# Router logits summed quarter by quarter from rows not yet normalised, with the first tiles routed apart

## The chip, the cores and the metric

The kernel runs on one core of one Trainium2 chip. The time is the device time of one execution in microseconds (us). An engine works through its own instructions in the order of the program: PE is TensorE, DVE is VectorE, ACT is ScalarE, POOL is GpSimd and SP is the queue that issues the direct DMAs. PEld is the loading of a matmul's stationary operand. PEclk is the clock of TensorE that was granted, as a share of full speed.

## What is computed

One step of a hybrid decoder layer for a prompt of 512 rows and 8 sample rows, all of width 1024. A mixing sublayer and a memory cross-attention come first. The change concerns the seam between the cross-attention's output projection, the layer norm behind it, and the routing of the mixture of experts. From the reference, cut to that:

```python
hp = layer_norm(ALPHA * hp + cross_attention(hp, mk_p, mv_p, w_xq[l], w_xo[l]), ln2_g[l], ln2_b[l])
hp = layer_norm(ALPHA * hp + hier_moe(hp, *moe_w), ln3_g[l], ln3_b[l])
...
def hier_moe(h, w_grp, b_grp, w_rtr, b_rtr, w_e_gate, w_e_up, w_e_down):
    grp_logits = jnp.einsum('td,dg->tg', t, w_grp)                 # 4 groups
    g_idx = jnp.argmax(grp_logits + b_grp, axis=-1)
    p_g = jnp.take_along_axis(jax.nn.softmax(grp_logits, axis=-1), g_idx[:, None], axis=1)
    e_logits = jnp.einsum('td,de->te', t, w_rtr)                   # 4 x 8 experts
    ...                                                            # top 2 inside the group g_idx
    for e in range(N_EXPERTS):
        he = jax.nn.silu(t @ w_e_gate[e]) * (t @ w_e_up[e])
        y = y + gates[:, e:e + 1] * (he @ w_e_down[e])
```

The logits of a row are 36 numbers: 4 of groups and 32 of experts. The 32 experts' weights are 192 units of 512 KB and are read once.

## The kernel before

The 520 rows are five tiles: 0 to 3 are the prompt's rows, 128 each, and 4 holds the 8 sample rows. The work is written as generators ("streams") that a planner interleaves by an estimate of TensorE's time: a stream yields the time, or the condition, from which it may go on, and among those that may, the one of the lowest priority number goes first. The planner's choice is the order of the program, and so the order on every engine.

`out_proj("wxo", ...)` (L1354) projects the cross-attention's output through `natural` (L416). It goes through four quarters q of 256 output columns. In each it takes the sample rows first (8 matmuls in full float32, two passes each) and then tiles 0 to 3, with 24 matmuls each in a reduced format of float32 (the operands are split into a high and a low part, so three products for each of 8 slices of the contraction). `put` adds the residual and takes the statistics of the quarter. After the last quarter of a tile, `finish(t)` normalises the tile on VectorE (`normalize`, L1344), stores its rows to the DRAM buffer `h2d` and adds a stream `rate(t)`.

`rate(t)` (L1652) makes the logits of one tile: eight transposes of the normalised rows in two PSUM banks, two copies to SBUF (ScalarE and VectorE), eight matmuls with the 36 router columns `wrt`, which accumulate in one bank, and two additions of biases (`logits` for the weights of the experts, `biased` for the choice). When all five tiles are rated the streams end and the routing follows in one piece for all tiles:

```python
    o = first_max(eb4, 4, 8)
    ...
    V.tensor_tensor(h, og4, o, op=OP.mult)     # one-hot of the k-th expert of each row
    ...
    ixg = M([16], I32, keep=True)
    V.tensor_scalar(ixg, ps[:, :16], BIG, None, op0=OP.add)
    ...
    for pr in range(2):
        gather(pr)
    ...
    warm(2)
    turn(0)
```

`first_max` finds the first largest of each group, twice, on VectorE; an element of its operands is one expert of one tile, so 160 elements wide. Small matmuls count for each chosen expert how many rows stand ahead of this one (`pp`, `rank`), `placed` turns the ranks into a list `ixg` of row numbers for 16 pairs of experts, and `gather` (L1841) has POOL fetch the rows of a pair from `h2d` by an indirect DMA. `warm(n)` issues n matmuls whose results nobody uses. `turn(0)` transposes the gathered rows, and `gate_up(0)` multiplies them with the first pair's weights.

The experts' weights come in units of 512 KB (1024 columns). `prefetch` (L1627) issues a load for each free block of SBUF whenever blocks become free, in the order in which they are used. A last region (`arena_l`, nine units) becomes free when the projection's own buffers close. From `gate_up(0)` on, blocks are freed as the products use them up (`drop`), and the loads go on.

## Time and profile before

| what | value |
|---|---|
| median of 3 runs | 908.75 us (905.33 to 913.02) |
| the profiled execution, its time | 907.26 us |
| the profiled execution, its span | 905.5 us |
| mean granted clock of TensorE | 0.951 |
| busy share of the span: PE, DVE, ACT, POOL | 91%, 54%, 33%, 10% |
| chain that ended last, share by engine | PE 62%, DMA 22%, DVE 8%, ACT 3%, issue 2%, SPq 2% |
| read from HBM | 223.11 MB |

The time of the profiled execution lies 1.8 us above its span. A busy share is a mean over stages with different limits. The chain names what released each step, going back from the last instruction.

### The profile page before, as it was taken

The page shows a single profiled execution, that of the slowest core. Times are in us where ns is not written, and L with a number is a line of the kernel's source. Part 1 is how long each engine was busy: PE and PEld are TensorE (multiplying, and loading weights), DVE is VectorE, ACT ScalarE, POOL GpSimd, SP SyncE. Part 2 cuts the span into 40 slices and gives each one's busy share as a digit, 9 for nine tenths or more (in the row PEclk, how much of TensorE's full clock was granted, in tenths as well). Part 3 has the DMA queues.
Part 4 walks back from the last instruction along what each step waited for, and adds up shares of the span by engine and source line. Part 5 has one row for each costly group of instructions (what it writes and reads, how often), then busy time and mean ns, then how long its engine had stood idle before and what let it go on. Part 6 is the DMA issues. An engine that isn't in the chain of part 4 may idle for free.

```text
span 905.5 us, 17155 instructions
## 1 busy us (share of the span) xinstructions
PE 820.4 (91%) x6767; PEld 575.3 (64%) x6767; DVE 485.7 (54%) x1079; ACT 294.4 (33%) x616; POOL 87.5 (10%) x88
## 2 busy tenths in 40 slices
PE   6999989999997898999989989996899989989982
PEld 6998556666875786898768965995343434334331
DVE  5565356675557554533651675567453834625635
ACT  5422334352632433420442342121232403313311
POOL 4100101111320000000000001000310210200100
PEclk9999999999997987999979999998899999989997
DMA  7922696766793576688867346228699999999950
GB/s 265 310 80 79 178 281 203 247 196 230 231 350 132 192 256 233 228 307 318 268 218 278 98 162 209 84 107 313 209 409 411 412 409 410 408 409 409 409 210 24
DMA packets 83960, 230.43 MB, mean 254 GB/s; under 512 B 12482, under 2 KB 32988, under 8 KB 83492
## 3 DMA queue, kind: packets, MB, share of 16 engines
q1 hardware_dynamic: 74660, 203.98, 62.7%
q0 software_dynamic: 9216, 25.31, 8.0%
q8 instruction: 55, 0.90, 0.4%
q14 instruction: 29, 0.24, 0.1%
HBM read 223.11 MB, written 14.39 MB: 262 GB/s over the span
## 4 chain that ended last, share of the span: by engine, by line
PE 62%; DMA 22%; DVE 8%; ACT 3%; issue 2%; SPq 2%; POOL 0%; POOLq 0%; ACTq 0%; DVEq 0%
PE psd L219 33%; DMA arena_f<-in_we 10%; PE psm L219 9%; PE psx L219 9%; PE pss L219 7%; DVE arena_f L200 5%; DMA arena_d<-in_we 4%; PE psm L223 3%; DMA arena_l<-in_we 2%; DVE arena_r L200 2%; DMA arena_f<-in_latT 2%; ACT arena_f L200 2%; ACT arena_r L200 1%; SPq L239 1%; DMA arena_f<-in_wuq 1%
## 5 line engine op out<-in xcount | busy, mean ns | idle before, releaser
L219 PE MATMUL psd<-arena_r 128*128 128x256 f32 (+1 forms) x2208 | 295.9, 293 | 9.0 <-ACT arena_r L200 5.6
L219 PEld LDWEIGHTS psd<-arena_r 128*128 128x128 f32 x2208 | 281.7, 198 | 21.5 <-issue 9.3
L219 PE MATMUL psx<-arena_f 96*32 96x256 f32 (+1 forms) x728 | 132.7, 495 | 2.2 <-DMA arena_f<-in_latT 1.9
L200 DVE TENSOR_TENSOR arena_r<-arena_f,arena_r 128x1024 fp32r<-128x1024 f32 (+3 forms) x71 | 83.0, 1173 | 77.3 <-ACT arena_r L200 71.7
L200 ACT CAST arena_r<-arena_f 128x1024 fp32r<-128x1024 f32 (+3 forms) x73 | 71.2, 977 | 159.2 <-PE psd L219 118.7
L219 PE MATMUL psm<-arena_f 64*32 64x32 f32 (+10 forms) x1394 | 87.1, 282 | 14.4 <-DVE arena_f L200 9.4
L219 PE MATMUL pss<-arena_f 128*8 128x256 f32 (+5 forms) x466 | 92.3, 466 | 1.3 <-ACT arena_f L200 0.7
L219 PEld LDWEIGHTS psx<-arena_f 96*32 96x32 f32 (+1 forms) x728 | 43.9, 125 | 68.5 <-issue 51.9
L223 PE MATMUL psm<-cst,arena_f 128*128 128x128 f32 (+2 forms) x393 | 59.9, 280 | 19.8 <-DVE arena_f L200 5.4
L219 PEld LDWEIGHTS psm<-arena_f 64*32 64x32 f32 (+6 forms) x1384 | 47.6, 123 | 46.2 <-issue 22.5
L223 PEld LDWEIGHTS psm<-cst,arena_f 128*128 128x128 f32 (+2 forms) x393 | 44.0, 148 | 44.1 <-issue 20.4
L200 DVE TENSOR_TENSOR arena_f<-arena_f 128x1024 f32<-128x1024 f32 (+6 forms) x72 | 57.2, 827 | 7.5 <-ACT arena_f L200 3.6
L219 PEld LDWEIGHTS pss<-arena_f 128*8 128x8 f32 (+3 forms) x456 | 30.3, 121 | 37.8 <-issue 26.7
L200 DVE TENSOR_TENSOR arena_f<-arena_f,psx 128x256 f32<-128x256 f32 (+1 forms) x17 | 7.4, 432 | 86.9 <-ACT arena_f L200 86.9
L638 POOL DMA_INDIRECT arena_f<-in_latN,ixn x32 | 34.3, 1073 | 189.9 <-PE psm L219 176.2
L200 DVE SCALAR_TENSOR_TENSOR arena_f<-arena_f,psd 128x256 f32<-128x256 f32 (+2 forms) x60 | 28.6, 489 | 43.9 <-PE psd L219 34.6
L1841 POOL DMA_INDIRECT arena_f<-h2d,arena_s x24 | 26.2, 1092 | 220.8 <-PE psm L223 123.6
L200 ACT ACTIVATE arena_f<-psx 128x256 f32<-128x256 f32 x16 | 6.1, 384 | 122.8 <-PE psx L219 117.5
L219 PE MATMUL psx<-arena_d,arena_f 128*64 128x512 f32 x76 | 37.1, 676 | 9.4 <-DMA arena_d<-in_we 9.4
L219 PE MATMUL pss<-arena_l,arena_f 128*64 128x512 f32 x92 | 43.2, 593 | 0.0
L219 PE MATMUL psx<-arena_l,arena_f 128*64 128x512 f32 x92 | 35.7, 596 | 5.2 <-DMA arena_l<-in_we 5.2
L200 DVE SCALAR_TENSOR_TENSOR arena_m<-pss,arena_s,arena_m 128x512 fp32r<-128x512 f32 x32 | 23.7, 750 | 29.7 <-ACT arena_m L200 29.7
(212 smaller groups left out, 919.8 us busy)
## 6 DMA issues: line engine op xcount, KB each, us to landing
arena_f<-in_we SPq DMA_DIRECT2D x120, 512.0 KB, 10.6
arena_l<-in_we SPq DMA_DIRECT2D x46, 512.0 KB, 10.8
arena_f<-in_latT SPq DMA_DIRECT2D x128, 144.0 KB, 2.9
arena_d<-in_we SPq DMA_DIRECT2D x26, 512.0 KB, 11.1
arena_f<-in_wout SPq DMA_DIRECT2D x16, 512.0 KB, 5.5
arena_f<-in_wxq SPq DMA_DIRECT2D x16, 512.0 KB, 5.4
arena_f<-in_memKT SPq DMA_DIRECT2D x16, 512.0 KB, 5.3
arena_f<-in_memV SPq DMA_DIRECT2D x16, 512.0 KB, 5.2
```

The costliest lines, as they stand in the source:

```text
L200: return f(out, *args, **kw)
L219: return self.queue(self.eng.matmul(out, lhsT, rhs, **kw))
L223: return self.queue(self.eng.transpose(out, src, ident))
L239: return self.eng.dma_start(out, src)
L638: G.indirect_dma_start(out=out, out_offset=None, in_=src, in_offset=bass.IndirectOffsetOnAxis(ap=ix, axis=0))
L1841: G.indirect_dma_start(out=out, out_offset=None, in_=h2d, in_offset=bass.IndirectOffsetOnAxis(ap=ix, axis=0), bounds_check=NT - 1, oob_is_ ...
```

## The change

Four things change.

`rate(t, q)` now runs for each quarter of each tile, as soon as the quarter's residual is there. It transposes two blocks of the raw rows (not yet normalised), copies them to SBUF (ScalarE for even quarters, VectorE for odd ones), multiplies them with the two matching slices of `wrt` and adds the 36 sums into `logits`. The normalisation is put right afterwards: with mean m and reciprocal deviation r of a row, its logits are r times (raw sum minus m times the column sum of `wrt`) plus the bias. `prepare` makes the negative column sum (`moe["sum"]`) with eight more matmuls. At the last quarter the rows are normalised on ScalarE (Identity with scale and bias) instead of VectorE and stored.

The routing is split. `ORDER` is (0, 1, 4, 2, 3). A new stream `route()` waits until tile 3 is projected and tiles 0, 1 and 4 are rated, and chooses their experts (`choose(0, 3)`). The last step of tile 3's rating waits for that and emits the ranks of the first three tiles ahead of its own last logit matmuls. Behind the streams come `choose(3, 2)` for tiles 2 and 3 and their ranks, whose matmuls accumulate on the counts of the first three.

The bursts of warming matmuls are 2, 1 and 6 where there was one of 2.

A region of small buffers, `arena_s`, grows from 1400 to 1600 columns, and `arena_f` next to it loses none.

```diff
-COLS_S = 1400
+COLS_S = 1600
...
+            if then:
+                then(t, q)
...
+    ORDER = (0, 1, 4, 2, 3)
+    PLACE = [ORDER.index(t) for t in range(5)]
...
+    def rate(t, q):
         o, n = tiles5[t]
-        slots = moe["xt"].slots
-        if not slots:
-            yield lambda: slots
-        h2T = slots.pop(0)
-        for c in range(2):
-            ps = pm()
-            for k in range(4):
-                f = 4 * c + k
-                PE.transpose(ps[:, k * 128:k * 128 + n], res[t][:n, f * 128:(f + 1) * 128], ident[:n, :n])
-            to, p3 = h2T[:, 4 * c:4 * c + 4, :n], ps.rearrange("p (k n) -> p k n", k=4)[:, :, :n]
-            if c:
-                V.tensor_copy(to, p3)
-            else:
-                S.copy(to, p3)
-        yield PE.ready()
-        ps = ps_()
-        for k in range(8):
-            PE.matmul(ps[:n, :36], h2T[:, k, :n], moe["wrt"][:, k], start=k == 0, stop=k == 7)
-        V.tensor_add(biased[:n, t], ps[:n, :36], moe["bias2"][:n])
-        V.tensor_add(logits[:n, t], ps[:n, :36], moe["bias"][:n])
-        slots.append(h2T)
+        if "slots" not in moe or not moe["slots"]:
+            yield lambda: moe.get("slots")
+        h2T = moe["slots"].pop(0)
+        ps = pm()
+        for k in range(2):
+            f = 2 * q + k
+            PE.transpose(ps[:, k * 128:k * 128 + n], res[t][:n, f * 128:(f + 1) * 128], ident[:n, :n])
+        (V.tensor_copy if q % 2 else S.copy)(h2T[:, :, :n], ps[:, :256].rearrange("p (k n) -> p k n", k=2)[:, :, :n])
+        if q == 3:
+            mv, rs = moe["moments", t]
+            shift = stat.tile([128, 1], F32, tag="shift", name="shift", bufs=5)
+            V.scalar_tensor_tensor(shift[:n], mv[:n, 0:1], -1.0, rs[:n], op0=OP.mult, op1=OP.mult)
+            S.activation(res[t][:n], res[t][:n], AF.Identity, bias=shift[:n], scale=rs[:n])
+            Q.dma_start(h2d[o:o + n, :], res[t][:n])
+        yield PE.ready() if q == 3 else PE.now + 2.5
+        if q == 3 and "sum" not in done:
+            yield after("sum")
+        if (t, q) == (3, 3):
+            yield after("chosen")
+            ranks_of_first()
+        lg, p = moe["lg"][:n, t * 36:t * 36 + 36], PLACE[t]
+        if q == 3:
+            V.scalar_tensor_tensor(logits[:n, p], moe["sum"][:n], mv[:n, 0:1], logits[:n, p], op0=OP.mult, op1=OP.add)
+        for k in range(2):
+            PE.matmul(lg, h2T[:, k, :n], moe["wrt"][:, 2 * q + k], start=k == 0, stop=k == 1)
+        moe["slots"].append(h2T)
+        if q == 0:
+            V.tensor_copy(logits[:n, p], lg)
+        else:
+            V.tensor_add(logits[:n, p], logits[:n, p], lg)
+        if q < 3:
+            return
+        V.scalar_tensor_tensor(biased[:n, p], logits[:n, p], rs[:n], moe["bias2"][:n], op0=OP.mult, op1=OP.add)
+        V.scalar_tensor_tensor(logits[:n, p], logits[:n, p], rs[:n], moe["bias"][:n], op0=OP.mult, op1=OP.add)
         done.add(("rated", t))
-            normalize(t, 4)
-            Q.dma_start(h2d[o:o + n, :], res[t][:n])
-            streams.add(rate(t), -1, PE.now + 3.8)
-        yield from out_proj("wxo", columns2(hh, hl), xs, range(8), finish, lambda t: crossed)
+            moe["moments", t] = moments(t, 4)
+            done.add(("projected", t))
+        yield from out_proj("wxo", columns2(hh, hl), xs, range(8), finish, lambda t: crossed,
+                            lambda t, q: streams.add(rate(t, q), -1, PE.now + (0.0 if q == 3 else 2.5)))
...
+        moe["lg"] = ps_()
+        moe["slots"] = [xt[:, 2 * i:2 * i + 2] for i in range(4)]
+        yield PE.now + 9.0
+        ps = ps_()
+        for k in range(8):
+            PE.matmul(ps[:, :36], ones, moe["wrt"][:, k], start=k == 0, stop=k == 7)
+        V.tensor_scalar(moe["sum"], ps[:, :36], -1.0, None, op0=OP.mult)
+        done.add("sum")
...
+    def choose(a, m):
+        sl = slice(a, a + m)
+        b3 = biased[:, sl, 4:36]
+        b4 = b3.rearrange("p t (g e) -> p t g e", g=4)
+        for k in range(2):
+            o = first_max(b4, 4, 8, a, m)
+            if k == 0:
+                first_max(biased[:, sl, None, 0:4], 1, 4, a, m)
+                V.scalar_tensor_tensor(b3, o.rearrange("p t g e -> p t (g e)"), -3e38, b3, op0=OP.mult, op1=OP.add)
+            V.tensor_tensor(OH[k][:, sl].rearrange("p t (g e) -> p t g e", g=4), moe["og4"][:, sl], o, op=OP.mult)
...
+    def ranks(a, m):
+        sl = slice(a, a + m)
+        t32, rank = moe["t32"][:, sl], moe["rank"]
+        for k in range(2):
+            V.tensor_mul(t32, OH[k][:, sl], (moe["ahead"] if a else pp())[:, :m * 32].rearrange("p (t e) -> p t e", t=m))
+            V.reduce_sum(rank[:, sl, k], t32, axis=AX.X)
+            V.tensor_tensor(RR[k][:, sl], C("iota64")[:, None, :].to_broadcast([128, m, 64]),
+                            rank[:, sl, k:k + 1].to_broadcast([128, m, 64]), op=OP.is_equal)
+    def ranks_of_first():
+        ps = pp()
+        for k in range(2):
+            PE.matmul(ps[:, :96], moe["ub"], OH[k][:, :3].rearrange("p t e -> p (t e)"), start=k == 0, stop=False)
+            for p in range(3):
+                n = tiles5[ORDER[p]][1]
+                if p < 2:
+                    PE.matmul(ps[:, p * 32 + 32:96].rearrange("p (t e) -> p t e", e=32), moe["onesb"][:n],
+                              OH[k][:n, p:p + 1].to_broadcast([n, 2 - p, 32]), start=False, stop=k == 1 and p == 1)
+                PE.matmul(moe["ahead"][:, :64].rearrange("p (t e) -> p t e", e=32), moe["onesb"][:n],
+                          OH[k][:n, p:p + 1].to_broadcast([n, 2, 32]), start=k + p == 0, stop=False)
+        ranks(0, 3)
...
+    def route():
+        yield after(("projected", 3), *(("rated", t) for t in ORDER[:3]))
...
+        choose(0, 3)
+        for k in range(2):
+            carried(k, moe["tk"], 0, 3)
+        done.add("chosen")
...
+    placed_of(0, 3)
+    warm(2)
+    choose(3, 2)
+        PE.matmul(moe["ahead"][:, :64], moe["ub"], OH[k][:, 3:5].rearrange("p t e -> p (t e)"), start=False, stop=False)
+        PE.matmul(moe["ahead"][:, 32:64], moe["onesb"], OH[k][:, 3], start=False, stop=k == 1)
+    warm(1)
     for k in range(2):
-        val = carried(k, moe["tk"])
-        V.tensor_mul(t32, OH[k], pos)
-        V.reduce_sum(rank[:, :, k], t32, axis=AX.X)
-        rr = R(64, dt=BF)
-        V.tensor_tensor(rr, C("iota64")[:, None, :].to_broadcast(BC + [64]),
-                        rank[:, :, k:k + 1].to_broadcast(BC + [64]), op=OP.is_equal)
-        RR.append(rr)
-        placed(ps, k, val, k == 0, k == 1)
+        carried(k, moe["tk"], 3, 2)
+    ranks(3, 2)
+    placed_of(3, 2)
...
-    warm(2)
+    warm(6)
     turn(0)
```

On TensorE, this is the second quarter (q = 1) of the output projection. `psd<-arena_r` are the projection's matmuls, `psm<-cst` the transposes, `pss<-arena_s,arena_f 128x36` the logits of a quarter and `pss<-arena_s,ones` the column sum:

```order
-L219 MATMUL psd<-arena_r 128x256 x96
+L219 MATMUL psd<-arena_r 128x256 x24
+L219 MATMUL pss<-arena_s,arena_f 128x36 x2
+L223 MATMUL psm<-cst,arena_f 128x128 x2
+L223 MATMUL psm<-cst,arena_f 128x8 x2
+L219 MATMUL pss<-arena_s,ones 128x36 x8
+L219 MATMUL psd<-arena_r 128x256 x24
+L219 MATMUL pss<-arena_s,arena_f 128x36 x2
+L219 MATMUL pss<-arena_s,arena_f 8x36 x2
+L223 MATMUL psm<-cst,arena_f 128x128 x2
```

One unbroken row of 96 projection matmuls becomes four of 24, with transposes and logits of other tiles between them; over the four quarters the places at which such a row is cut go from 3 to 11.

On TensorE, the end of the projection and what stands behind it, before the change:

```order
-L219 MATMUL psd<-arena_r 128x256 x24
-L219 MATMUL pss<-arena_s,arena_f 128x36 x8
-L223 MATMUL psm<-cst,arena_f 128x128 x8
-L219 MATMUL pss<-arena_s,arena_f 128x36 x8
-L223 MATMUL psm<-cst,arena_f 128x128 x8
-L219 MATMUL pss<-arena_s,arena_f 128x36 x8
-L219 LDWEIGHTS arena_s
-L219 MATMUL psm<-arena_s 128x160
```

And now (`psd<-arena_s 128x96` is the first matmul of `ranks_of_first`):

```order
+L219 MATMUL psd<-arena_r 128x256 x24
+L219 MATMUL pss<-arena_s,arena_f 128x36 x2
+L223 MATMUL psm<-cst,arena_f 128x128 x2
+L219 MATMUL pss<-arena_s,arena_f 128x36 x2
+L219 LDWEIGHTS arena_s
+L219 MATMUL psd<-arena_s 128x96
```

Behind the last 24 matmuls stood logits and transposes of three tiles; now three pairs of logits and one pair of transposes are left. Eleven more matmuls of the ranks follow the last row shown, and only behind them comes the third pair, the last of tile 3.

On VectorE, the stretch that begins with the residual of tile 3's last quarter (`psd`) in the order after the change:

```order
+L200 SCALAR_TENSOR_TENSOR arena_f<-arena_f,psd 128x256
+L200 TENSOR_TENSOR arena_s<-arena_s,pss 128x36
+L200 BN_STATS arena_s<-arena_f 128x6
+L200 SCALAR_TENSOR_TENSOR arena_s<-arena_s,lrs 128x36
+L200 BN_AGGR mv<-arena_s 128x2
+L200 COPY arena_f<-psm 128x256
+L200 RECIPROCAL lrs<-lrs 128x1
+L200 SCALAR_TENSOR_TENSOR arena_s<-arena_s,lrs 128x36
+L200 SCALAR_TENSOR_TENSOR shift<-mv,lrs 128x1
+L200 TENSOR_REDUCE arena_f<-arena_s 128x12
+L200 TENSOR_REDUCE arena_f<-arena_s 128x3
```

The two reductions at the end open `choose(0, 3)`. They stand behind tile 3's statistics (the residual, the two BN rows, the reciprocal and `shift`), with the last logits of tile 2 in between. On SP the loads of the weights keep their order around the seam, except that one of the two `arena_l` loads ahead of tile 3's store to `h2d` now stands behind it.

## Rows read from the trace of the kernel before

**Rows 1.** Windows: us, busy time (instructions) of each engine, granted clock, DMA share, GB/s.

```profile
60.00:240.00 180.00, 171.40 (x1462) 121.24 (x1461) 100.23 (x287) 70.46 (x167) 21.14 (x23) 0.97 0.63 198
634.00:645.00 11.00, 8.00 (x28) 2.56 (x28) 5.34 (x26) 3.24 (x6) 3.05 (x3) 0.76 0.31 92
680.00:840.00 160.00, 148.72 (x678) 61.01 (x678) 78.84 (x144) 45.09 (x92) 20.38 (x18) 0.97 1.03 410
870.00:880.00 10.00, 10.00 (x46) 3.34 (x46) 0.87 (x2) 1.07 (x2) 0.00 (x0) 1.00 0.18 73
```

**Rows 2.** Timeline of SP's queue: start, us, line, operation, out<-in, count.

```profile
619.38 0.33 SPq L239 DMA_DIRECT2D h2d<-arena_f  x1
619.75 4.36 SPq L239 DMA_DIRECT2D arena_l<-in_we  x7
624.21 21.43 SPq L239 DMA_DIRECT2D arena_f<-in_we  x4
...
644.83 4.24 SPq L239 DMA_DIRECT2D arena_f<-in_we  x6
```

**Rows 3.** Timeline of TensorE, end of the projection, rating, warming (x counts passes).

```profile
585.46 11.77 PE L219 MATMUL psd<-arena_r 128*128 128x256 f32 x96
597.15 1.05 PE L219 MATMUL psd<-arena_f,arena_s 128*8 128x256 f32 x16
...
611.13 1.07 PE L223 MATMUL psm<-cst,arena_f 128*128 128x128 f32 x8
611.96 3.13 PE L219 MATMUL psd<-arena_r 128*128 128x256 f32 x24
614.93 1.87 PE L219 MATMUL pss<-arena_s,arena_f 128*128 128x36 f32 x16
616.63 1.07 PE L223 MATMUL psm<-cst,arena_f 128*128 128x128 f32 x8
...
621.16 1.98 PE L219 MATMUL pss<-arena_s,arena_f 128*128 128x36 f32 x16 [0.29 <-ACT arena_f L200]
...
631.71 3.78 PE L219 MATMUL psx<-arena_f,cst 128*128 128x512 f32 x4
```

**Rows 4.** Timeline of VectorE: residual and normalising of tile 3, then the routing.

```profile
615.12 0.42 DVE L200 SCALAR_TENSOR_TENSOR arena_f<-arena_f,psd 128x256 f32<-128x256 f32 x1 [1.97 <-PE psd L219]
...
618.54 0.81 DVE L200 TENSOR_SCALAR arena_f<-arena_f,mv,lrs 128x1024 f32<-128x1024 f32 x1
...
623.41 0.40 DVE L200 TENSOR_REDUCE arena_f<-arena_s 128x20 f32<-128x160 f32 x2
...
624.12 0.17 DVE L200 TENSOR_TENSOR arena_s<-arena_s 128x20 f32<-128x20 f32 x1
...
627.65 0.32 DVE L200 TENSOR_TENSOR arena_s<-arena_f 128x160 bf16<-128x160 f32 x1
```

**Rows 5.** The chain that ended last, in order of time: start, us, what.

```profile
633.15 5.04 DMA arena_f<-h2d,arena_s
...
639.56 8.67 PE psx L219 x32
...
651.93 7.04 PE psx L219 x32
```

**Rows 6.** Timeline of TensorE in an earlier projection, large and small matmuls in turn.

```profile
415.88 1.05 PE L219 MATMUL pss<-arena_f 128*8 128x256 f32 x16
416.86 1.69 PE L219 MATMUL psd<-arena_r,arena_c 128*128 128x256 f32 x12
...
419.91 0.62 PE L219 MATMUL pss<-arena_f 128*8 128x256 f32 x8
420.46 1.69 PE L219 MATMUL psd<-arena_r,arena_c 128*128 128x256 f32 x12
```

**Rows 7.** A window inside the first gate-and-up product.

```profile
640.00:641.00 1.00, 1.00 (x4) 0.24 (x2) 1.00 (x6) 0.82 (x2) 0.65 (x1) 0.50 0.00 0
```

**Rows 8.** DMA issues in 600 to 905 us: median us from issue to landing at the end.

```profile
arena_f<-h2d,arena_s POOLq DMA_INDIRECT x24, 7.4
```

More of the change, by code (lines that the diff above doesn't have):

```diff
@@ L1731, in prepare @@
         del raws[2:]
+        moe["lg"] = ps_()
+        moe["slots"] = [xt[:, 2 * i:2 * i + 2] for i in range(4)]
         prefetch()
-    def tail():
-        yield after("recurrence", ("gate", 4))
-        AF_.free(kpe, wgate, qkS)
-    for prio, gen in enumerate((paged(), attention(), recurrence(), misc(), queries(), keys(), step(), sample(), values(), mixing(), memory(), first(), cross_queries(), prepare(), second(), tail())):
-        streams.add(gen, prio)
-    for h in range(4):
-        streams.add(cross_head(h), 20 + h)
-    streams.run()
-    BC = [128, 5]
-    AF_.free(moe["wrt"])
-    AT = Arena(moe["rest"], REST)
-    AT.more = AF_.small
-    xt = AT.get(8, 128)
+        yield PE.now + 9.0
[4 more added lines that the diff above has]
+        done.add("sum")
+    OH, VAL, RR = [], [], []
     def M(shape, dt=F32, rows=128, keep=False):
         n = math.prod(shape)
-        v = (AF_ if keep else AT).get(-(-n // 2) if dt == BF else n, rows=rows)
+        v = (AF_ if keep else moe["AT"]).get(-(-n // 2) if dt == BF else n, rows=rows)
         if dt != F32:
@@ L1801, in tile_hybrid_decoder_step @@
-    AT.free(runs[4])
-    pos = pp[:, :160].rearrange("p (t e) -> p t e", t=5)
-    rank = R(2, keep=True)
-    VAL, RR = [R(2, 4, 16, dt=BF) for _ in range(2)], []
-    t32 = R(32)
-    ps = pm()
-    def placed(ps, k, val, start, stop):
-        for t, (_, n) in enumerate(tiles5):
-            for q in range(2):
-                PE.matmul(ps[64 * q:64 * q + 64, :math.prod(val.shape[3:])], RR[k][:n, t],
-                          val[:n, t, q].rearrange("p j c -> p (j c)"), start=start and t == 0, stop=stop and t == 4)
@@ new lines, in tail @@
+    def tail():
+        yield after("recurrence", ("gate", 4))
+        AF_.free(kpe, wgate, qkS)
+    for prio, gen in enumerate((paged(), attention(), recurrence(), misc(), queries(), keys(), step(), sample(), values(), mixing(), memory(), first(), cross_queries(), prepare(), second(), route(), tail())):
+        streams.add(gen, prio)
+    for h in range(4):
+        streams.add(cross_head(h), 20 + h)
+    streams.run()
+    xt = moe["xt"]
+    xgs, ohr, yhr, iota = (moe[n] for n in ("xg", "oh", "yh", "iota"))
```

119 lines of the change are left out of this document (62 added, 57 removed).

## The prediction

> **What bounds the kernel now.** I read the table of windows first, then the chain of waits, then the timelines of PE, VectorE and the DMA queue around 585 to 650 us. From about 650 us to about 870 us the expert weights stream in at 410 GB/s with a DMA share of 1.03, and at 870 us the share has dropped to 0.18 [rows 1]. What follows is a tail that depends on the last weights, so the kernel ends a fixed time after that stream ends, and the stream ends a fixed time after it resumes. It has to resume because it stands still: between 634 and 645 us the DMA share is 0.31 [rows 1], since every free block of SBUF already holds weights. The queue row says when it goes on: the load behind the four of 624.21 is issued at 644.83 us [rows 2], when the first gate-and-up product of expert pair 0 has released blocks. So the time of the kernel moves by as much as this first release moves, as long as memory is full before it.
>
> Going backwards from the release, the chain of waits gives the gather of rows at 633.15 (5.04 us), then turning, then gate-and-up at 639.56, which takes 8.67 us where the next takes 7.04 [rows 5]; the granted clock in 640 to 641 us is 0.50 [rows 7]. Ahead of the gather, VectorE's first choosing operation stands at 623.41 and the second one-hot is written by 627.97 (627.65 + 0.32) [rows 4]: 4.56 us, then 5.18 us to the gather. Ahead of that TensorE has no gaps: the last projection matmuls run from 611.96 to 614.93, and rating of tiles 1, 2 and 3 to 623.14 [rows 3]. The last quarter of the projection, 597.15 to 614.93, is 17.78 us, although its 96 large matmuls need 11.69 (585.46 to 597.15) [rows 3]. The rest is rating that already lies there: tiles 4 and 0, and the transposes of tile 1.
>
> **What is moved ahead of the last projected tile.** A tile's eight logit matmuls take 1.70 us (614.93 to 616.63), its eight transposes 0.83 (611.13 to 611.96) [rows 3]. From behind the last projection the change takes forward the logits of tile 1 (1.70) and transposes and logits of tiles 2 and 3 (2 x 2.53), and it adds the eight matmuls of the column sum, of the same shape as a tile's logits (1.70): 8.46. Behind it stay three of the twelve quarter pairs of logits (3 x 0.425 = 1.28) and one pair of transposes (0.21). So 8.46 - 1.49 = +7.0 us of matmuls are now in front. Nothing hides them, because TensorE is the engine that is full there.
>
> The order also shows that the runs of 96 projection matmuls are cut into pieces of 24. There were 3 cuts in four quarters and there are 11: 8 more. The price of a cut is read where large and small matmuls alternate earlier: 16 small ones take 0.98 (415.88 to 416.86), 8 take 0.55 (419.91 to 420.46), so 8 more of them cost 0.43; the period with 8 is 3.60 (416.86 to 420.46), of which 24 large ones are 24 x 11.69/96 = 2.92, and 3.60 - 2.92 - 0.43 leaves 0.25 [rows 3, 6]. I take 0.28 with the handshake of a shorter group: 8 x 0.28 = +2.2. The last projection then ends 7.0 + 2.2 = **+9.2 us** later, at 624.1. The bounds are +8.1 (cuts at half price) and +10.5 (the new groups also wait now and then for the copy that feeds them).
>
> **From the last projection to the gather.** Before, this is 633.15 - 614.93 = 18.2 us. After, the order has VectorE work through the statistics of tile 3 first. From the residual at 615.12 to the normalising at 618.54 these take 3.42 in the trace [rows 4], with two additions and a PSUM copy of other tiles between them; without about 0.7 of those, 2.7. Only then comes the first reduction of the first three tiles: it stands behind tile 3's statistics on the same engine.
> A dependent operation costs by its width. 20 elements take 0.17 and 160 take 0.32 [rows 4], so 96 take 0.25 and 64 take 0.22. The twelve dependent operations of one choosing took 4.56, that is 0.38 each, 0.06 above the busy time. For three tiles: 12 x 0.31 = 3.7, with the group's small operations 4.1. For two: 12 x 0.28 = 3.4, with those 3.7.
> Between the two choosings lie the ranks' last matmuls, tile 3's last pair of logits and the handshakes (1.3: three of about 0.43) and the correction by mean and bias (0.7: four narrow operations of 0.17). From the second one-hot to the gather it was 5.18; most operations are now 64 wide instead of 160, so 4.3, with 3.5 and 5.5 as ends. Sum: 2.7 + 4.1 + 1.3 + 0.7 + 3.7 + 4.3 = 16.8, that is **-1.4**, with -2.7 and +0.5 as ends. The eight us of rating that left this stretch are nearly all taken up again by a second chain of choosing.
>
> [...]
>
> **Behind the gather.** The gather starts at -1.4 + 9.2 = +7.8. Six warming matmuls instead of two now fill TensorE while the gather runs. If they bring the clock to full, gate-and-up takes 7.04 instead of 8.67 [rows 5]: **-1.6**. The gather lies beside more loads than before. SP must issue tile 3's row store before the last weight loads. It went out at 619.38, 4.45 after the last projection, and 7 + 4 loads behind it had landed by about 634, 14.6 later [rows 1, 2]. In the order of after, one load more stands behind this store (1.3 more). So memory is full at about 624.1 + 4.5 + 14.6 + 1.3 = 645, and the gather, from 641, shares the DMA for some 4 us instead of about 1. Beside a busy stream a gather lands in 7.4 [rows 8] against this one's 5.04. I take **+1.0**, between 0 and +2.4. Since 645 is still ahead of the new release (644.8 + 7.2 = 652), the release decides as before, and a shorter stall of the DMA in itself gives nothing back: the stream waits for the same blocks.
>
> **What costs nothing.** Normalising goes to ScalarE, which has little else there, and is off the chain, except through the store named above. The larger small arena moves stores and transposes of the first 240 us forward by some ten groups. TensorE is busy 171.4 of 180 us between 60 and 240 [rows 1], so all the idle time that such a move could win or double is 8.6; I take 0, between -3 and +3.
>
> **The sum.** +9.2 - 1.4 - 1.6 + 1.0 = **+7.2**. The profiled execution took 907.26, its span 905.5 and 1.8 around it: 907.26 + 7.2 = **914.5**. The three runs' median is 1.5 above the profiled one and their lowest 1.9 below, so I add nothing for that.
>
> **Rival B: the first choosing really lies under the projection.** The change's words promise this. If the first three tiles are chosen while tile 3 is still projected, the stretch behind the last projection is statistics 2.7, a pair of logits 0.4, correction 0.7, choosing 3.7 and rest 4.3 = 11.8 instead of 16.8. That gives 914.5 - 5.0 = 909.5, and with the cheaper end of the projection (+8.1) and of the gather (0) 907.4: not slower. It decides where VectorE gets to the first reduction before the statistics of tile 3. Against it speaks that the reduction stands behind tile 3's shift in VectorE's order, and an engine works in its order; for it only that waits, not work, fill VectorE there. Chance 0.15, a fifth of it below 899.7 with gains in the first 240 us.
> [...]
>
> **Rival C: the six warming matmuls run at the low clock.** They stand on TensorE ahead of the turning of the gathered rows. In the trace two of them took 3.78 [rows 3], 1.9 each, after an idle stretch; so six would be 11.3, from about 0.5 before the gather. The gather lands some 6 after its start, the turning would wait 4.8 more, and the first product could still start slow: 914.5 + 5 to 6 = 920. At twice that speed they are 5.7 and hidden. It decides where one takes more than about 1.1. For it: TensorE again waits for VectorE's choosings, as it did before the row of 3.78. Against it: the four matmuls of the ranks and two bursts of warming come closer together now. Chance 0.15.
>
> **How the numbers follow.** The forecast, 914.5, has a chance of 0.70, B 0.15, C 0.15. Its own range, from the ends above taken together (not all at one end), is 908 to 920. For 8 in 10 I go to 904 below, for B with a gain early on, and to 922 above, for C with a late gather. One per cent, 9.1 us, is about what a measurement can tell from no change; the limits are 899.7 and 917.8. Forecast: 0.02 faster, 0.48 within, 0.20 slower. B: 0.03 faster, 0.12 within. C: 0.15 slower. Sum: 0.05, 0.60, 0.35.
>
> **What would show it.** In the profile after: the last 24 projection matmuls end at 624 (a wrong first term if before 622 or after 626); the first 96-wide reduction on VectorE starts some 2.7 later and not before that end (else B); the second one-hot lies about 9.8 behind the first reduction; the gather starts at 641; the six warming matmuls take under 6 us (else C); the first gate-and-up takes about 7.0; the DMA's stall ends at about 652. The time before 590 us should be as before to within 3 us. The prediction is wrong at its root if memory is not yet full when the first blocks are released, since then the release no longer decides the end.

## The result, and the profile after

The changed kernel takes 920.12 us (median of four runs, 916.15 to 924.77), the kernel before 907.68 in the runs beside it (905.33 to 913.02): a ratio of 1.012, with a 95% interval of 1.0081 to 1.0159. It is 1.2% slower. The profiled run is the slowest of the four (924.77, span 922.9), so the rows below stand for a difference of 17.4 us between the spans, where the medians differ by 12.4.

The windows of the kernel after, over the same stages as [rows 1]: us, busy time (instructions) of PE, PEld, DVE, ACT and POOL, granted clock, DMA share, GB/s.

```profile
60.00:240.00 180.00, 170.80 (x1437) 121.87 (x1439) 98.77 (x281) 66.66 (x161) 19.90 (x26) 0.95 0.61 191
650.00:655.00 5.00, 4.79 (x12) 1.81 (x10) 4.49 (x18) 0.21 (x1) 3.00 (x2) 1.00 0.91 334
655.00:660.00 5.00, 4.22 (x24) 1.99 (x26) 3.00 (x13) 3.07 (x5) 0.98 (x1) 1.00 0.32 94
690.00:850.00 160.00, 151.16 (x697) 66.87 (x694) 79.22 (x143) 46.56 (x95) 21.78 (x19) 0.98 1.03 410
886.00:896.00 10.00, 10.00 (x40) 3.12 (x38) 0.42 (x1) 0.38 (x1) 0.00 (x0) 0.83 0.24 97
565.70:633.81 68.11, 66.18 (x588) 61.46 (x588) 35.10 (x107) 16.32 (x26) 1.21 (x2) 1.00 0.25 83
```

The last row is the cross-attention's output projection, from its first matmul to its last. Before, its window and its first row in TensorE's timeline were:

```profile
557.35:614.93 57.58, 57.50 (x522) 54.09 (x522) 33.65 (x79) 9.70 (x15) 1.21 (x2) 1.00 0.30 101
557.35 1.05 PE L219 MATMUL psd<-arena_f,arena_s 128*8 128x256 f32 x16
```

The stages are the old ones: a stall of the DMA (0.32 in 655 to 660), the stream at 410 GB/s, the tail. The tail's clock is new: 0.83 against 1.00 in [rows 1].

SP's queue in the timeline after: tile 3's store, most of the last loads that still find free blocks, the first loads behind the stall, and the last load of all.

```profile
637.34 0.32 SPq L239 DMA_DIRECT2D h2d<-arena_f  x1
637.70 5.85 SPq L239 DMA_DIRECT2D arena_l<-in_we  x8
...
660.55 4.24 SPq L239 DMA_DIRECT2D arena_f<-in_we  x6
...
881.92 0.33 SPq L239 DMA_DIRECT2D arena_l<-in_we  x1
```

The last load before:

```profile
866.19 0.33 SPq L239 DMA_DIRECT2D arena_l<-in_we  x1
```

TensorE in the timeline after: the projection's start, a piece of it with its cuts, its end, the ranks, the warming matmuls, the turning and the first gate-and-up.

```profile
565.70 1.05 PE L219 MATMUL psd<-arena_f,arena_s 128*8 128x256 f32 x16
...
587.72 1.98 PE L219 MATMUL pss<-arena_s,ones 128*128 128x36 f32 x16
589.53 3.11 PE L219 MATMUL psd<-arena_r 128*128 128x256 f32 x24
592.48 0.53 PE L219 MATMUL pss<-arena_s,arena_f 128*128 128x36 f32 x4
593.30 0.30 PE L219 MATMUL pss<-arena_s,arena_f 128*8 128x36 f32 x4 [0.29 <-DVE arena_s L200]
593.52 0.44 PE L223 MATMUL psm<-cst,arena_f 128*128 128x128 f32 x2
593.72 3.13 PE L219 MATMUL psd<-arena_r 128*128 128x256 f32 x24
596.68 0.53 PE L219 MATMUL pss<-arena_s,arena_f 128*128 128x36 f32 x4
597.05 0.41 PE L223 MATMUL psm<-cst,arena_f 128*128 128x128 f32 x2
597.22 3.13 PE L219 MATMUL psd<-arena_r 128*128 128x256 f32 x24
...
633.81 0.53 PE L219 MATMUL pss<-arena_s,arena_f 128*128 128x36 f32 x4
...
638.22 0.59 PE L219 MATMUL psd<-arena_s 128*128 128x96 bf16 x6 [2.94 <-DVE arena_s L200]
...
649.38 5.42 PE L219 MATMUL psx<-arena_f,cst 128*128 128x512 f32 x12
655.67 1.09 PE L223 MATMUL psm<-cst,arena_f 128*128 128x128 f32 x8 [0.88 <-DMA arena_f<-h2d,arena_s]
656.87 7.09 PE L219 MATMUL psx<-arena_f 128*64 128x512 f32 x32
```

VectorE's timeline after: the residual of tile 3's last quarter, the first reduction of `choose(0, 3)`, the second one-hot of `choose(3, 2)`.

```profile
634.00 0.42 DVE L200 SCALAR_TENSOR_TENSOR arena_f<-arena_f,psd 128x256 f32<-128x256 f32 x1 [1.82 <-PE psd L219]
...
635.89 0.32 DVE L200 TENSOR_REDUCE arena_f<-arena_s 128x12 f32<-128x96 f32 x2
...
646.09 0.22 DVE L200 TENSOR_TENSOR arena_s<-arena_f 128x64 bf16<-128x64 f32 x1
```

POOL's timeline after: the first gather.

```profile
650.73 2.01 POOL L1910 DMA_INDIRECT arena_f<-h2d,arena_s  x1 [83.83 <-DMA arena_l<-in_we]
```

Read from the start of this projection the two traces part as follows. It lasts 633.81 - 565.70 = 68.11 us, before 614.93 - 557.35 = 57.58: **+10.53**. From its end to the gather it is 16.92 instead of 18.22 (-1.30), from there to the turning 4.94 instead of 5.17 (-0.23), and the first gate-and-up takes 7.09 instead of 8.67 (-1.58). That sums to +7.4. The first load behind the stall goes out at 660.55 instead of 644.83 [rows 2]: +15.72, of which 8.35 is a later start of the whole projection and 7.37 is this seam. From that load to the issue of the last one it is 221.37 us after (881.92) and 221.36 before (866.19). That the two agree to a hundredth is chance: in the profiles of the other kernels below that hold no loads back it is 220.5 to 223.2. So the release decides the stream's end to within some 3 us. Behind it the tail is 40.98 instead of 39.31.

### The profile page after: what moved, and what is told of

Its sections match the earlier page's. It is cut to its first block, busy times and chain, and to the rows that moved or that the text cites. A ratio compares the mean times of both kernels' runs of the same rounds, so it can differ in the third digit from the quotient of the medians.

```text
span 922.9 us, 17300 instructions
## 1 busy us (share of the span) xinstructions
PE 836.3 (91%) x6803; PEld 587.6 (64%) x6803; DVE 489.4 (53%) x1139; ACT 301.8 (33%) x626; POOL 86.9 (9%) x90
## 5 line engine op out<-in xcount | busy, mean ns | idle before, releaser
L219 PE MATMUL psd<-arena_r 128*128 128x256 f32 (+1 forms) x2208 | 299.7, 294 | 9.0 <-ACT arena_r L200 5.4
L219 PE MATMUL psm<-arena_f 64*32 64x32 f32 (+9 forms) x1384 | 90.9, 290 | 13.3 <-DVE arena_f L200 8.1
L219 PE MATMUL pss<-arena_f 128*8 128x256 f32 (+4 forms) x466 | 91.5, 461 | 2.0 <-DMA arena_f<-in_memV 1.4
L219 PEld LDWEIGHTS psm<-arena_f 64*32 64x32 f32 (+6 forms) x1384 | 49.9, 125 | 48.4 <-issue 26.8
L223 PE MATMUL psm<-cst,arena_f 128*128 128x128 f32 (+2 forms) x389 | 62.2, 283 | 20.0 <-ACT arena_f L200 5.3
L200 DVE TENSOR_TENSOR arena_f<-arena_f 128x1024 f32<-128x1024 f32 (+8 forms) x75 | 57.6, 799 | 6.9 <-ACT arena_f L200 4.0
L219 PEld LDWEIGHTS pss<-arena_f 128*8 128x8 f32 (+3 forms) x456 | 29.9, 120 | 37.4 <-issue 25.6
L219 PE MATMUL psx<-arena_d,arena_f 128*64 128x512 f32 x76 | 40.0, 721 | 5.9 <-DMA arena_d<-in_we 5.9
## 6 DMA issues: line engine op xcount, KB each, us to landing
arena_f<-in_we SPq DMA_DIRECT2D x120, 512.0 KB, 10.5
arena_d<-in_we SPq DMA_DIRECT2D x26, 512.0 KB, 10.5
```

The source lines that it names most:

```text
L200: return f(out, *args, **kw)
L219: return self.queue(self.eng.matmul(out, lhsT, rhs, **kw))
L223: return self.queue(self.eng.transpose(out, src, ident))
```

## The experiments

The table holds every kernel's times, read in its one profile in the same way; ratios are to the kernel before, run beside it on the same chip.

| kernel | projection starts | lasts | end to gather | gather to turning | first gate-and-up, to the next matmul | projection's end to last load issued | last load to end | ratio (95%) |
|---|---|---|---|---|---|---|---|---|
| before | 557.4 | 57.58 | 18.22 | 5.17 | 8.50 | 251.3 | 39.3 | 1 |
| after | 565.7 | 68.11 | 16.92 | 4.94 | 6.92 | 248.1 | 41.0 | 1.012 (1.008 to 1.016) |
| e1_cols_only | 554.2 | 57.56 | 18.23 | 4.94 | 8.33 | 250.2 | 39.3 | 1.002 (0.999 to 1.004) |
| e2_seam_only | 559.7 | 68.10 | 17.31 | 4.94 | 6.92 | 249.7 | 41.1 | 1.016 (1.012 to 1.019) |
| e3_quarters_only | 558.4 | 68.09 | 13.80 | 8.26 | 8.62 | 250.7 | 41.1 | 1.017 (1.013 to 1.022) |
| e4_split_only | 555.3 | 57.59 | 18.22 | 6.13 | 7.98 | 251.2 | 39.4 | 1.001 (0.998 to 1.004) |
| e5_filler | 562.1 | 68.13 | 18.23 | 5.19 | 8.31 | 250.5 | 39.3 | 1.011 (1.006 to 1.016) |
| e6_warm6_only | 560.0 | 57.59 | 18.23 | 5.96 | 6.92 | 249.7 | 39.3 | 0.999 (0.996 to 1.001) |
| e7_grouped | 565.3 | 82.70 | 17.05 | 6.16 | 6.91 | 251.3 | 39.3 | 1.023 (1.018 to 1.029) |
| e8_two_first | 565.2 | 68.09 | 12.76 | 8.29 | 8.68 | 250.8 | 41.1 | 1.015 (1.011 to 1.020) |
| e9_two_first_hold | 561.1 | 68.09 | 12.63 | 4.97 | 6.91 | 251.1 | 39.4 | 1.013 (1.009 to 1.018) |
| e10_whole_two_first_hold | 561.2 | 57.57 | 18.63 | 4.84 | 6.92 | 254.1 | 41.0 | 1.005 (1.002 to 1.009) |
| e11_two_first_hold4 | 568.9 | 68.11 | 12.75 | 5.02 | 6.92 | 245.7 | 39.4 | 1.010 (1.007 to 1.014) |

### Where the loss is: the early stretch or the seam

**e1_cols_only**: the kernel before with the larger small arena, which moves stores and transposes of the first 240 us.

```diff
-COLS_S = 1400
+COLS_S = 1600
```

> The kernel before with arena_s at 1600 columns and nothing else changed. It separates the early part (the projection of the cross-attention began 8.35 us later in the profile after than in the one before) from the seam. Theory (the order in the first 240 us really got worse with the larger arena): 3 to 7 us slower than before, and the output projection of the cross-attention begins 4 to 9 us later than at 557.35. Rival (that slip is the scatter of single executions, or belongs to the seam): within 2 us of before, beginning within 3 us of 557.35.

Measured: 908.94 against 909.04. The move of the early groups costs nothing that can be told. Ahead of the projection the two traces show the same order on TensorE and on SP here and in the kernel after, and yet the projection begins at 554.2 here and at 565.7 there.

**e2_seam_only**: the changed kernel with an arena of 1464 columns, with which the first 240 us are ordered as before.

```diff
-COLS_S = 1600
+COLS_S = 1464
```

> The kernel after with arena_s at 1464 columns, at which the order of all engines ahead of the projection is that of before. Theory (seam and early order each cost their own part): about 7.4 us slower than before (projection +10.5, from its end to the gather -1.3, first gate-and-up -1.6, gather -0.2), with the projection beginning within 3 us of 557.35 and lasting 68 us. Rival (the arena's size does nothing): 12 us slower, as the kernel after.

Measured: 921.39 against 909.04, all of the loss. A theory that gave the arena a part of it falls; what is done around the seam carries it.

### Which part of the seam

**e3_quarters_only**: quarter by quarter as in e2, but all five tiles are chosen in one go (the bursts of 2 and 1 warming matmuls go with the second choosing).

```diff
-        if (t, q) == (3, 3):
-            yield after("chosen")
-            ranks_of_first()
...
-        yield after(("projected", 3), *(("rated", t) for t in ORDER[:3]))
+        yield after(("projected", 3), *(("rated", t) for t in ORDER))
...
-        choose(0, 3)
...
+    choose(0, 5)
+    ranks_of_all()
```

> As the one before it (arena_s 1464), but with one routing of all five tiles behind the projection: quarter by quarter rating alone. Theory (two chains of choosing cost about 3.3 us more than one): the projection lasts 68 us, its end to the gather 13.6 us (2.7 statistics, 1.1 last logits and correction, 4.6 choosing, 5.2 to the gather), so about 4 us slower than before and 3 us faster than with the split. Rival (the split costs nothing, since the first choosing stands where VectorE would wait): the stretch is 16 to 17 us and the time as in the seam alone.

Measured: 922.41 against 909.04. The stretch to the gather shrinks to 13.80, 3.5 less than in e2, and nothing comes of it, since the gather now takes 8.26 to the turning. The windows of e3 show what it shares the DMA with:

```profile
640.00:645.00 5.00, 5.00 (x9) 2.04 (x8) 4.52 (x20) 0.21 (x1) 2.91 (x2) 0.66 1.03 417
645.00:648.00 3.00, 1.51 (x4) 0.38 (x2) 0.38 (x2) 0.00 (x0) 0.00 (x0) 1.00 0.96 374
648.00:649.00 1.00, 0.44 (x4) 0.47 (x5) 0.00 (x0) 0.00 (x0) 0.00 (x0) 1.00 0.26 98
```

The weight loads queued ahead of it run out at 648; the turning begins at 648.56, 22.06 behind the projection's end. In the kernel after, 3.1 us slower to the gather, it is 21.86. So the choosing in one go comes out as expected (13.6), and the 3 us that were expected from it do not.

**e4_split_only**: the split routing as in e2, but tiles are rated whole, from normalised rows, as before (with a second buffer for transposed blocks, and no column sum).

```diff
-    def rate(t, q):
+    def rate(t):
...
-        lg, p = moe["lg"][:n, t * 36:t * 36 + 36], PLACE[t]
+        lg, p = ps_(), PLACE[t]
...
-            moe["moments", t] = moments(t, 4)
+            o, n = tiles5[t]
+            normalize(t, 4)
+            Q.dma_start(h2d[o:o + n, :], res[t][:n])
...
+            streams.add(rate(t), -1, PE.now + 3.8)
```

> As the seam alone (arena_s 1464), but the rating is that of before (whole tiles of normalised rows, normalised on VectorE, no column sum) and only the routing is split; the last logits of tile 3 stand behind the first choosing in VectorE's order only. Theory (the split pays where TensorE still rates tiles 2 and 3): the projection lasts 57.6 us as before, the first choosing starts about 617.5 and ends under the rating of tile 3, the gather comes about 2 us earlier than 18.2 behind the projection, the first gate-and-up takes 7.1: about 3.5 us faster than before. Rival (two chains of choosing cost more than the rating hides): gather 0 to 2 us later, time within 2 us of before.

Measured: 908.64 against 909.04. With whole tiles the projection is 57.59 again and the loss is gone, but the split gains nothing, neither the 2 us to the gather nor the 3.5 in all that were expected: end to gather is 18.22, as before to a hundredth.

**e5_filler**: the kernel before with four warming matmuls behind tile 1 in three of the quarters, to make the projection as long as it is after and do nothing else.

```diff
...
+        def filler(t, q):
+            if q and t == 1:
+                ps = px()
+                for _ in range(4):
+                    PE.matmul(ps, ident, moe["iota"][:, :512], start=True, stop=True)
+
-        yield from out_proj("wxo", columns2(hh, hl), xs, range(8), finish, lambda t: crossed)
+        yield from out_proj("wxo", columns2(hh, hl), xs, range(8), finish, lambda t: crossed, filler)
```

> The kernel before with twelve matmuls added whose results nobody uses, four behind tile 1 in each of quarters 1 to 3 of the cross output projection; rating, routing and loads as before. Twelve by 0.90 (six took 5.42 in the profile after) is 10.8, and three more cuts 0.8: the projection lasts 69 us instead of 57.6. Theory (the end of the projection carries through to the end of the kernel one to one, whatever the work in it is): 11 to 13 us slower than before. Rival (the DMA's standstill of ten us before the first release takes up part of a later projection, and what the change costs comes from the routing): 0 to 6 us slower.

Measured: the projection is 68.13 (+10.55), the time 922.72 against 911.99, a difference of medians of 10.7 (5.6 to 14.9 by the interval of the ratio). In the profiles the last load goes out 250.5 behind the projection's end and 251.3 before. Time on TensorE ahead of the projection's end is paid one to one within this interval, whatever fills it.

**e6_warm6_only**: the kernel before with six warming matmuls instead of two.

```diff
-    warm(2)
+    warm(6)
```

> The kernel before with six warming matmuls ahead of the first turning instead of two, nothing else changed. Theory (they hold the clock up over the gather): the first gate-and-up takes 7.1 instead of 8.67 and the time is 1 to 2 us less, at the edge of what five rounds tell. Rival (after the choosing's idle TensorE the six themselves run at the low clock, 1.9 us each, and delay the turning): the six take 8 to 11 us and the time is 2 to 6 us more.

Measured: 910.37 against 911.99, within what can be told. TensorE's timeline of e6 has the six in one row:

```profile
634.35 7.57 PE L219 MATMUL psx<-arena_f,cst 128*128 128x512 f32 x12
```

Gate-and-up gains 1.6 and the turning comes 0.8 later, so about half of the gain is left at the release (29.1 behind the projection's end instead of 29.9). Behind the second choosing, in the kernel after, the same row takes 5.42.

### Can the cut be made cheaper?

**e7_grouped**: as e2, but a quarter's pairs are rated together behind the quarter's last tile, to cut the large runs in fewer places.

```diff
+        def rate_later(t, q):
+            if q == 3:
+                streams.add(rate(t, q), -1, PE.now)
+            elif t == 3:
+                for i in (4, 0, 1, 2, 3):
+                    streams.add(rate(i, q), -1, PE.now + 2.5)
...
+                            rate_later)
```

> The seam alone (arena_s 1464) with the ratings of quarters 0 to 2 done together behind the quarter's last tile instead of behind each tile; quarter 3 as it was. The matmuls are the same, the runs of projection matmuls are cut in 8 places instead of 11. Theory (a cut costs 0.28, and in the profile after TensorE waited up to 0.5 for copies in each of some ten groups): the projection lasts 66 to 67.5 us instead of 68.1, time 0 to 2 us less than the seam alone. Rival (nearly all of the 10.5 us are cuts and waits, not matmuls): 63 to 65 us and 3 to 5 us less.

Measured: 934.97 against 911.99; the projection takes 82.70 and both theories fall. In TensorE's timeline the large runs are cut in 10 places instead of 11, not in the 8 that both expected, so the run does not tell what a cut costs. Two other things are seen there and in the windows of e7:

```profile
587.60 4.60 PE L219 MATMUL psd<-arena_r 128*128 128x256 f32 x24
...
593.83 0.61 PE L219 MATMUL pss<-arena_s,arena_f 128*128 128x36 f32 x4 [0.38 <-DVE arena_s L200]
594.81 0.94 PE L219 MATMUL pss<-arena_s,arena_f 128*128 128x36 f32 x4 [0.38 <-DVE arena_s L200]
...
595.88 4.19 PE L219 MATMUL psd<-arena_r 128*128 128x256 f32 x24
...
600.27 3.12 PE L219 MATMUL psd<-arena_r 128*128 128x256 f32 x24
...
638.09 5.14 PE L219 MATMUL psd<-arena_r 128*128 128x256 f32 x24
```

```profile
595.00:600.00 5.00, 5.00 (x32) 5.00 (x31) 0.20 (x1) 0.37 (x1) 0.00 (x0) 0.67 0.01 3
600.00:603.00 3.00, 3.00 (x28) 3.00 (x27) 0.90 (x3) 1.01 (x1) 0.00 (x0) 1.00 0.01 3
638.00:643.00 5.00, 5.00 (x27) 5.00 (x26) 0.85 (x2) 2.61 (x3) 0.00 (x0) 0.53 0.57 216
565.34:648.04 82.70, 75.93 (x587) 69.29 (x587) 36.07 (x107) 15.77 (x26) 1.20 (x2) 0.90 0.20 68
```

The pairs stand in a row and each waits for the last one's sum. Then, with TensorE in short matmuls and waits before it, the 24 large ones take 4.19 at a granted clock of 0.67, where they take 3.12 at 1.00. Later in the same projection a row of 24 (638.09) takes 5.14, at 0.53. Over the whole projection TensorE idles 6.77 us instead of the 1.93 of the kernel after, and is busy 75.93 instead of 66.18 with the same matmuls.

### Can the choosing really lie under the projection?

**e8_two_first**: as e2, with `ORDER` (0, 4, 1, 2, 3); only tile 0 and the sample rows are chosen first, and VectorE may do it ahead of tile 3's last quarter.

```diff
-    ORDER = (0, 1, 4, 2, 3)
+    ORDER = (0, 4, 1, 2, 3)
...
-        yield after(("projected", 3), *(("rated", t) for t in ORDER[:3]))
+        yield after(*(("rated", t) for t in ORDER[:2]))
...
+    streams.add(route(), -2)
...
-    choose(3, 2)
+    choose(2, 3)
```

> The seam alone (arena_s 1464) with tiles 0 and 4 as the first set and 1, 2 and 3 as the second, and with the first choosing free to run before the projection has ended: in VectorE's order it stands ahead of tile 3's last residual. This is the rival of the prediction in which a choosing really lies under the projection. If it pays in full, the stretch from the projection's end to the gather falls from 17.3 to about 13 and the time by about 4 us against the seam alone, to 8 us above before. Theory: the gather does start about 4 us earlier, but its rows land behind the loads of weights that the end of the projection let go (as in the run with one routing, where it took 8.3 us), so the first release moves by less than 2 us and the time is that of the seam alone within 2 us.

Measured: 925.57 against 911.99. VectorE does begin at 631.33, 1.9 ahead of the projection's end (633.25), and the gather comes 12.76 behind that end, 4.2 earlier than after. It is all lost again. TensorE's timeline of e8 (the warming, the turning, gate-and-up), then windows of one us:

```profile
644.57 6.18 PE L219 MATMUL psx<-arena_f,cst 128*128 128x512 f32 x12
...
654.30 1.97 PE L223 MATMUL psm<-cst,arena_f 128*128 128x128 f32 x8 [3.54 <-DMA arena_f<-h2d,arena_s]
...
656.20 8.86 PE L219 MATMUL psx<-arena_f 128*64 128x512 f32 x32
```

```profile
652.00:653.00 1.00, 0.00 (x0) 0.00 (x0) 0.00 (x0) 0.00 (x0) 0.00 (x0) 0.99 1.04 406
653.00:654.00 1.00, 0.00 (x0) 0.00 (x0) 0.00 (x0) 0.00 (x0) 0.00 (x0) 0.50 0.94 357
654.00:655.00 1.00, 0.70 (x4) 0.71 (x5) 0.00 (x0) 0.00 (x0) 0.00 (x0) 0.50 0.18 62
```

The gather, issued at 646.01, lands about when the loads run out, at 654. TensorE waits 3.54 for it, is granted 0.50 and pays 1.8 more for gate-and-up.

**e9_two_first_hold**: e8, but only 7 loads are let through at the projection's end (5 of them go out behind it); the next 7 wait until the gathered rows have landed.

```diff
-    def prefetch():
+    def prefetch(most=99, behind=None):
-        while parts:
+        while parts and most:
...
+            most -= 1
+            if behind is not None:
+                G.tensor_copy(v[:, :1], behind[:, :1])
...
-        prefetch()
+        prefetch(7)
...
-        prefetch()
...
+    prefetch(behind=xgs[0])
```

> As the run with tiles 0 and 4 first (gather 12.75 behind the projection's end, its rows in TensorE's hands only 8.3 later, at the moment at which the DMA's stream of weights ran out), but only seven units of weights are loaded behind the projection; the others are held until the first gathered rows have landed (a small copy on GpSimd, from the gathered rows into each of their blocks, stands ahead of their loads). Theory (the queued loads are what the gather waits for): the rows land 5 to 5.5 after the gather's start, the first gate-and-up runs at full clock, the first release is 22 to 24 behind the projection's end instead of 28.4, and the time 3 to 5 us less than with tiles 0 and 4 first. Rival (the gather takes its 8 us for itself, for example in the making of its descriptors): landing unchanged, and the time the same or up to 5 us more, since loads are now late.

**e11_two_first_hold4**: the same with fewer loads held back (8 go out behind the projection's end, 4 wait); the edit is against e9.

```diff
-        prefetch(7)
+        prefetch(10)
```

> As the run with seven units held, but eight units are loaded behind the projection and four held. With seven held the DMA stood still before the gather instead of after it (the loads ran out about 639, the gather started 641.9, the held loads went out from 647.1), so the last load was issued 251.1 behind the projection's end, no earlier than with nothing held (250.8). Theory (what counts is the DMA's standstill from the projection's end on, wherever it lies): with four held the loads run out about when the gather starts, the rows land 5 to 6 after that, the standstill is 3 to 5 us instead of 8, the last load is issued 246.5 to 248.5 behind the projection's end, and the time is 2 to 4 us less than with seven held. Rival (the stream after the release sets its own pace and standstills ahead of it do not matter): last load 250 to 251.5 behind, same time as with seven held.

Measured: 923.32 against 911.58, and 917.33 against 908.11. The gather now takes 4.97 and 5.02, gate-and-up 6.9: the delay in e8 was the loads. But in e9 the DMA stands still elsewhere, as the windows between the last free load and the landing show, of e9 and then of e11:

```profile
639.00:647.00 8.00, 6.22 (x27) 2.71 (x27) 7.36 (x33) 0.21 (x1) 3.01 (x3) 1.00 0.46 150
```

```profile
646.00:655.00 9.00, 8.56 (x31) 3.52 (x29) 8.18 (x37) 0.21 (x1) 3.02 (x3) 0.80 0.89 329
```

A share of 0.46 over 8 us is a standstill of 4.3; 0.89 over 9 us is 1.0. An earlier landing alone is no earlier stream: the last load goes out 251.1 behind the projection's end in e9, no earlier than before, and 245.7 in e11. So what counts is the whole standstill of the DMA from that end on, wherever it lies. Over the stretch from that end to the last load the DMA moves 388 GB/s before, 390 in e9 and 397 in e11; at the stream's 410 that leaves an estimated standstill of 13.5, 12.3 and 7.8 us. e11 has the best seam of all, 5.6 us better than before, and still is 1% slower, since its projection is 10.5 longer. That makes 5.0 of the 9.2 us by which its median is slower (6.1 to 12.6 by the interval); the rest is not found in its seam or its tail.

**e10_whole_two_first_hold**: the same choosing and holding on whole tiles (e4), 9 loads let through.

```diff
-    ORDER = (0, 1, 4, 2, 3)
+    ORDER = (0, 4, 1, 2, 3)
...
-        prefetch()
+        prefetch(9)
...
```

> The same routing and the same holding of loads with the rating of before (whole tiles of normalised rows, no column sum): tiles 0 and 4 chosen under the projection's last tile, the weights beyond nine units held until the rows have landed. Theory (with the projection not lengthened, the shorter way to the gather pays once the loads are out of its way): projection 57.6, gather 16 to 17 behind its end, landing in 5 to 5.5, first release 26 to 27 behind the end instead of 29.9: 3 to 4 us faster than before. Rival (the release only moves the standstill of the DMA, and the held loads are late by as much as the release is early): within 2 us of before.

Measured: 916.29 against 911.58. The short projection is kept, but the gather is no earlier (18.63), so holding back loads only makes the DMA stand still, an estimated 14.9 us in all by the same reckoning (386 GB/s over 254.1 us). Neither of the two expectations gives the 4.7 by which it is slower (1.4 to 8.2 by the interval). No kernel tried here beats the one before by more than can be told.

## Why the prediction was right, and where its sizes were off

The forecast was slower by 7.2, 914.5; measured are 920.1, just past the upper end of its own range (908 to 920) and inside the wider one (904 to 922), and 1.2% instead of 0.8%. That is beyond the one per cent within which the prediction had put 0.60 of its chances; it had given 0.35 to more. Its mechanism stands: the release of the first blocks sets the end, the projection's end sets the release, and what the change moves ahead of that end is paid in full (e5 shows it without any of the change's code, e4 shows the loss gone without the quarters). The seam comes out at +7.4 beside +7.2, closer than its terms deserve: +1.3 on the projection and -1.2 on the gather cancel. And of the 12.4 by which the medians differ, 5.0 lie outside the sum.

- **Projection, +9.2: measured +10.53, the mis-sized term.** It came out at the upper bound. Waits were named there, for the copies that feed the groups; most of those seen are for VectorE's sums. TensorE's idle time within the projection is 68.11 - 66.18 = 1.93 after and 57.58 - 57.50 = 0.08 before, by windows of just these stretches: +1.85 is waiting, as in the row at 593.30, where the pair waits for VectorE to take up the sum of the last one. The rest, 8.68, is busy time: the 7.0 of the matmuls moved, and 1.7 more. A cut that does not wait can cost less than I took: 593.72 to 597.22 is 3.50, and 24 large ones (2.92), two logits (0.43) and two transposes (0.21) make 3.56. So I had one price for cuts of several kinds: one like this, behind which the next pair is ready, costs nothing that can be read, and others wait. The 1.7 is in neither kind: summed from start to start over the timeline, the transposes take 0.8 longer than in whole tiles, the projection's own matmuls 0.4, the sample rows' logits 0.3, the column sum and the logits of `wrt` 0.1 each. The cuts, forecast at 2.2, thus cost 3.6 in all. The column sum took 1.81 (forecast 1.70).
- **End to gather, -1.4: measured -1.30.** Its parts: first reduction 2.08 behind the end (2.7), second one-hot written 10.42 behind that (9.8), gather 4.42 behind that (4.3). That splitting the choosing costs is shown by e3 against e2: one choosing for five tiles is 3.5 shorter (17.31 to 13.80). Of this the chains themselves, from the first reduction to the second one-hot in VectorE's timelines, make 2.8 (3.99 and 3.59 in e2, 4.79 in e3), beside the 2.5 that the prediction took from the rows (an estimated 3.7 and 3.4 for two chains, 4.56 for one).
- **Gather, +1.0: measured -0.2.** The loads had run out as the gather landed (share 0.91, then 0.32), so nothing was lost; in e3 and e8, where the gather goes out earlier, it is lost, 3.1 and 3.1.
- **First gate-and-up, -1.6: measured -1.58.** The six warming matmuls took 5.42, so rival C did not happen. Its price is seen in part in e6, where they take 7.57.
- **The arena, 0:** e1 bears it out.
- **Rival B** did not happen in the changed kernel: the reduction stands 2.08 behind the projection's end. e8 makes it happen, and still nothing is gained, which the prediction had not seen. With loads queued as they are the turning begins 21.1 (e8) to 22.3 (e2) behind the projection's end, whether the routing takes 12.8 or 17.3. The price of rival B, 5.0, was wrong for that reason. Moving work beside the projection lengthened the fuller engine by 10.5, and the freed stretch ran into the loads.
- **Not in the sum.** The tail is 1.67 longer in the profile, and I had it fixed. TensorE's last gate-and-up begins at 885.70 behind an idle 2.02, as it does at 870.00 before behind the same 2.02, but now the granted clock is 0.83 in 886 to 896. e2, e3, e8 and e10 have the same longer tail, the others have not. And the projection begins 8.35 later in this profile, where the prediction had wanted the time before 590 as before to within 3. The order of work is not the cause: with the same order on TensorE and SP e1 begins it at 554.2, and with the order of before e5 and e6 begin it at 562.1 and 560.0 instead of 557.4. So most of the 8.35 is the spread of single executions; in these five the granted clock in 60 to 240 goes the same way (0.97 before and in e1, 0.96 in e5 and e6, 0.95 after). Over all profiles it begins at 554 to 562 in kernels that rate whole tiles and at 558 to 569 in those that rate quarters, so a part may still belong to the change: in medians e2's seam and tail (10.52 - 1.5 + 1.7 = 10.7) leave 1.6 of its 12.4, and those of the kernel after (7.4 + 1.7) leave 3.4. What that rest is, and why the tail is longer, stays open.

## What to carry to other kernels

In a kernel that ends a fixed time after a stalled stream, find the point that frees the stream's memory, and count one to one what a change adds to the full engine's work ahead of that point: a shorter chain from there to the release has to pay for it. Such shortening pays only until the next wait in line, here loads already queued ahead of the gather; look first at what would be late next. Do not cut long matmul runs on the engine that is full to feed one that is idle: a piece can be nearly free where the next one is ready, but here the moved matmuls themselves cost 7.0 of the 10.5 us, the waits for VectorE's sums and copies 1.85, and the longer busy time of small groups 1.7.

## What the runs showed of the hardware that was not expected

- A gather issued behind queued weight loads landed about when these ran out: 8.3 us (e3, e8) instead of 5.0 (e9, e11, the gather of e8 with loads held back). By the packets in the traces its first one starts 5.1 us behind its issue in e3 and e8, and 2.6 to 2.7 in all other kernels here. In the kernel after, loads are still under way then (share 0.91 in 650 to 655), so how queued loads delay a gather stays open.
- In e7 TensorE's granted clock was 0.67 (595 to 600) and 0.53 (638 to 643) behind stretches of short matmuls with waits of 0.27 to 0.38 us: 24 large matmuls take 4.19 and 5.14 us there instead of 3.12 at 1.00.
- The same tail ran with a granted clock of 0.83 (after) and 1.00 (before) behind the same idle of 2.02 us; no run here tells why.
